# First stage of a hybrid encoder kernel: a hand-set order on four engines, and norm weights spread by a product with ones

## Chip, cores and metric

One core of a Trainium2 chip. The metric is the device time of one execution in microseconds; lower is better. The time before is the median of three runs.

## What is computed

Two layers over 512 tokens of width 1024, float32. Each layer normalises x, projects it to 4040 columns, runs four head groups on them (latent attention, differential attention, sparse attention, short convolution), gates them and projects back. Cut to what the change touches:

```python
def _rmsnorm(x, g):
    y = x * rsqrt(mean(x * x, axis=-1) + 1e-6)
    return y * g

for l in range(2):
    h = _rmsnorm(x, norm_g[l])
    p = split(h @ w_in[l])          # first: a_cq 256, a_ckv 128, a_krope 32, and c_kidx 32, c_widx 8
    ...
    x = x + y @ w_out[l]
return _rmsnorm(x, final_g)
```

## The kernel before

Tokens lie in 4 tiles of 128 (t = 0 to 3), the 1024 features of x in 8 groups of 128, taken in pairs (q = 0 to 3, one pair of weights each). Nearly all products are done in three passes of a split float32 (a high part `wh` or the first half of a `big`, and a low part `wl`): the high part is a copy on ACT, the low part a subtraction. For weights, `split_w` copies on ACT (L106) and subtracts on DVE (L108) and POOL (L101); for what leaves PSUM, `split_ps` copies on ACT (L115) and subtracts on DVE (L116). A PSUM bank is free again after DVE's part.

The first stage of a layer computes 456 columns (`a_cq`, `a_ckv`, `a_krope`, `c_kidx`, `c_widx`) for all tiles; the latent attention and the index scores wait for them. Its steps are listed in the string `FIRST`, one word each:

- `l`t loads tile t of x (two DMAs for tile 0; for tile 0 the norm weights too, L245, 512 KB: the row of 1024 weights is read for each of the 128 partitions into `g0`), all on SP's queue.
- `w`q loads weight group q, `c`q splits it (`first_load`, `first_split`).
- `s`t squares tile t on ACT in two halves with a sum (L261), `n`t finishes the norm: a root on ACT (L278), five small steps on DVE (L279 to L283), then x * scale * g in two halves on DVE (L286).
- `e`t transposes the normalised tile on PE, 8 transposes in 4 banks of two (L302, tag `pt`, 2 banks), each evicted by L115 and L116 (`Hidden.fill`).
- two digits, `qt`, are 6 products of 456 columns for group q and tile t (`first_part`); with q = 3 the norms of the latent vectors of tile t follow (`first_norm`, L527 to L537).

The set `START` names the engines on which the instructions of this stage keep the order of the code in the first layer: only SP. On the others a scheduler sets the order, within a model of its own, and it may bring in what comes later in the program. ACT, DVE, PE and POOL each run their queue in order. A root on one element (L994, `warm`) stands ahead of the stage in the code.

After the stage come the full projections (128 columns of the output at a time, 24 products of 512 columns each, L127), mixed with the latent products.

Of the kernel before, what the change touches and what calls it, by code (L numbers as in the profile page):

```python
# [9 lines left out]
FT = mybir.dt.float32  # L10
# [3 lines left out]
AF = mybir.ActivationFunctionType  # L14
# [5 lines left out]
P = 128  # L20
S = 512
D = 1024
# [4 lines left out]
EPS = 1e-6  # L27
BIG = 1e30
MARK = -3e38
FIRST = ("l0 w0 l1 l2 w1 l3 w2 w3 s0 n0 s1 c0 e0 00 n1 s2 c1 e1 01 10 11 n2 s3 e2 c2 02 12 20 21 n3 e3 c3 03 13 22 23 30 31 32 33",  # L30
         "w0 w1 c0 c1 00 10 01 11 w2 w3 c2 c3 e2 20 30 02 12 21 31 e3 03 13 22 32 23 33")
NBIG = 20
PIECE = 256
# [8 lines left out]
SLOTS = ('qi ga0 bl ga1', 'is|bi df0 gb0', 'sp1 tb', 'sp0 gc0 gb1 df1', 'tc cv0', 'cv1 gc1', '')  # L42
PW = 9.0
INORDER = set()
START = {mybir.EngineType.SP}
FM = (456, 456)
LATE = ((3, 3),)
FW = (("wh", "wl"), WB)
# [17 lines left out]
def hybrid_trunk(ctx, tc, x_in, norm_g, w_in, qa_g, w_uq, kva_g, w_ukv, dlam, subg,  # L66
                 conv_w, w_out, rel_bias, final_g, c_oh, c_cosf, c_sinf, c_tok, c_ones, c_mask, out):
    nc = tc.nc
    sb = lambda name, bufs: ctx.enter_context(tc.tile_pool(name=name, bufs=bufs))
    const = sb("const", 1)  # L70
# [7 lines left out]
    sm = sb("small", 4)  # L78
# [3 lines left out]
    def bank(tag):  # L82
        return ps.tile([P, 512], FT, name=f"ps_{tag}", tag=tag, bufs=BANKS[tag])

    def big(dt=FR):
        return pb.tile([P, 2, 512], dt, name="big", tag="big")

    def flat(t):
        return t.rearrange("p a b -> p (a b)")

    def prob():
        return pp.tile([P, 512], FT, name="prob", tag="prob")

    def raw_tile():
        return pw.tile([P, 1024], FT, name="wr", tag="wr", bufs=WR)
# [55 lines left out]
    ident = const.tile([P, P], FT, name="ident")  # L151
# [91 lines left out]
    def load_g(src, g=None):  # L243
        g = flat(big(FT)) if g is None else g
        nc.sync.dma_start(g, src[None, :].to_broadcast([P, D]))  # L245
        return g

    class Norm:


        def __init__(self, x, g, early=False):
            self.x, self.g, self.early = x, g, early
            self.xn = flat(big(FT))
            self.ss = sm.tile([P, 4], FT, name="ss")
            self.n = 0

        def part(self, c):
            n, ss = self.n, self.ss
            self.n += 1
            jk = prob()  # L260
            nc.scalar.activation(jk[:, :c.stop - c.start], self.x[:, c], AF.Square, accum_out=ss[:, n:n + 1])  # L261
            if c.stop < D:
                if n == 0:
                    nc.vector.tensor_scalar(out=ss[:, 0:1], in0=ss[:, 0:1], scalar1=1.0 / D, scalar2=EPS,
                                            op0=OP.mult, op1=OP.add)
                else:
                    nc.vector.scalar_tensor_tensor(out=ss[:, n:n + 1], in0=ss[:, n:n + 1], scalar=1.0 / D,
                                                   in1=ss[:, n - 1:n], op0=OP.mult, op1=OP.add)
            if self.early:
                for a in range(c.start, c.stop, PIECE):  # L270
                    d = slice(a, a + PIECE)
                    nc.gpsimd.tensor_tensor(out=self.xn[:, d], in0=self.x[:, d], in1=self.g[:, d], op=OP.mult)
# [36 lines left out]


    def layer(l, hT, enter, after):
        wl_ = w_in[l].rearrange("(k p) c -> p k c", p=P)
        pcl = lambda j: pcol[:, l * 10 + j:l * 10 + j + 1]
# [108 lines left out]
        def pair(k, unit, v, gt, post):  # L422

            yf = prob()
            for half in range(2):
                box = {}
                for j in range(2):
                    for qb in (2 * half, 2 * half + 1):
# [10 lines left out]
                        if qb % 2:  # L439
                            def prod(j=j, half=half, box=box):  # L440
                                nb = 2 * half + 2
                                if j == 0:
                                    box["o"] = bank("o")
                                o = box["o"]
                                pts = box[j]
                                for kb in range(nb):
                                    c = P if kb == nb - 1 else 0
                                    mm3(o[:, c:256], [tuple(x[:, kb, j * 64:j * 64 + P] for x in v)
                                                      + tuple(x[:, kb, c:256] for x in pts)],
                                        start=j == 0 and kb == 0, stop=j == 1 and kb == nb - 1, skip=True)  # L450
                                return 0.33 * nb

                            late.append((now + LAG[1], prod))
                            if j == 1:
                                c = slice(half * 256, (half + 1) * 256)
                                for i, part in enumerate(post(box, half, yf[:, c], gt[:, c])):
                                    late.append((now + LAG[2] + BSTEP * i, part))
                                if half == 1:
                                    late.append((now + LAG[2] + BSTEP * i, lambda: yfin(k, yf) or 0))
# [458 lines left out]

        with tc.manual_schedule(engines=START) if START and l == 0 else nullcontext():
            for step in FIRST[l].split():  # L920
                a, b = step
                if a == "w":
                    first_load(int(b))
                elif a == "c":
                    first_split(int(b))
                elif a in "lsne":
                    enter(int(b), a)
                else:
                    first_part(int(a), int(b))
            if l == 0:  # L930
                load_params()
# [56 lines left out]
        ctx.enter_context(tc.manual_schedule(engines=INORDER))  # L988
    h = Hidden()
    x0 = {}  # L990
    g0 = raw_tile()

    warm = sm.tile([P, 1], FT, name="warm", bufs=1)
    nc.scalar.activation(warm, ident[:, 0:1], AF.Sqrt)  # L994

    def enter(t, what, h=h):
        if what == "e":
            h.fill(t, x0[t].xn)
        elif what == "n":
            x0[t].finish()  # L1000
        elif what == "s":
            x0[t].part(slice(0, 512))
            x0[t].part(slice(512, D))
        else:
            x = flat(big(FT))
            for n in range(2 if t == 0 else 1):
                c = slice(n * 512, (n + 1) * 512) if t == 0 else slice(0, D)
                nc.sync.dma_start(x[:, c], x_in[t * P:(t + 1) * P, c])
            if t == 0:
                load_g(norm_g[0], g0)  # L1010
            x0[t] = Norm(x, g0)

    for l in range(DEPTH):
        st = {"n": []}

        def after(t, c, x, l=l, st=st):
            if t == 0 and c.start == 0:
                st["g"] = load_g(final_g) if l + 1 == DEPTH else load_g(norm_g[l + 1], raw_tile())
                if l + 1 < DEPTH:
                    st["h"] = Hidden()  # L1020
            if c.start == 0:
                st["n"].append(Norm(x, st["g"], l + 1 == DEPTH))
            norm = st["n"][t]
            norm.part(c)
            if c.stop < D:
                return
            norm.finish()
            if l + 1 < DEPTH:
                nc.sync.dma_start(xs[t * P:(t + 1) * P, :], x)
                if t >= 2:  # L1030
                    st["h"].fill(t - 2, st["n"][t - 2].xn)
            else:
                for c in (slice(0, 512), slice(512, 1024)):
                    nc.sync.dma_start(out[t * P:(t + 1) * P, c], norm.xn[:, c])

        layer(l, h, enter, after)
        if l + 1 < DEPTH:
            h = st["h"]

            def enter(t, what, h=h, ns=st["n"]):  # L1040
                h.fill(t, ns[t].xn)
# [52 lines left out]
```

## Time and profile before

| | us |
|---|---|
| median of 3 runs | 682.03 (677.00 to 683.62) |
| profiled execution | 679.76 |
| its span | 678.0 |
| PE busy in the span | 622.1 |
| start of PE's first instruction | 13.84 |
| granted TensorE clock, mean | 0.99 |

The span runs from the first to the last instruction of the core; the execution's own time holds 1.8 us around it. Times in the timeline are us from the span's start, then the us that the row lasts; a row with "xN" is N instructions run after one another, and its time is the sum that they cover. A bracket says how long the engine sat idle ahead of the row and what released it. PE is the product engine (its rows' ends are modelled), ACT, DVE and POOL the three others that compute, SP the queue that issues the loads.

### The profile page before, as it was taken

Reading aid. Unit: us, or ns where it says so; the run is one execution under the profiler, and the core shown is the slowest. Engines: PE = TensorE matmul, PEld = TensorE weight load, DVE = VectorE, ACT = ScalarE, POOL = GpSimd, SP = SyncE. Lnnn points to the kernel's source line nnn. Section 1 sums busy time; section 2 is a strip of 40 time slices with the busy share of each in tenths; the row PEclk is TensorE's granted clock in tenths of the full one; section 3 lists DMA queues with packets and bytes.
Section 4 is the critical chain, followed back from the end, with each engine's and each line's share of the span. In section 5 each row is a group of like instructions: output and inputs, shape, how many; then the busy total and the mean of one; then the engine's idle time right before and its main releaser. Section 6 shows DMA issues by size and latency. Waiting matters only on the chain.

```text
span 678.0 us, 11037 instructions
## 1 busy us (share of the span) xinstructions
PE 622.1 (92%) x3599; PEld 533.6 (79%) x3607; DVE 487.4 (72%) x1441; ACT 364.6 (54%) x879; POOL 278.5 (41%) x408
## 2 busy tenths in 40 slices
PE   1999999789999898999989899999999999999994
PEld 1877787678789677899968687879878977789994
DVE  3767762599999796645395767779999959664536
ACT  6556583484552564554364566866545256355435
POOL 2375432315434343442431854242534344344255
PEclk9999999799999999999999999999999999999998
DMA  8446573763455411233253653457244641132203
GB/s 262 117 111 191 148 133 94 185 158 99 109 145 151 118 47 43 83 125 114 58 169 91 181 171 103 139 135 170 65 115 116 190 117 48 47 109 100 80 1 125
DMA packets 86697, 80.71 MB, mean 119 GB/s; under 512 B 7302, under 2 KB 73400, under 8 KB 86640
## 3 DMA queue, kind: packets, MB, share of 16 engines
q1 hardware_dynamic: 86640, 80.02, 42.4%
q8 instruction: 28, 0.46, 0.3%
q14 instruction: 29, 0.24, 0.1%
HBM read 65.22 MB, written 12.16 MB: 114 GB/s over the span
## 4 chain that ended last, share of the span: by engine, by line
PE 58%; DVE 26%; ACT 7%; DMA 5%; issue 2%; POOL 1%; SPq 0%; ACTq 0%; DVEq 0%; POOLq 0%
PE ps_proj L127 43%; PE ps_o L127 5%; DVE ia L595 5%; DVE m L594 4%; PE ps_pt L414 3%; PE ps_s L127 2%; DMA wr<-in_w_in_dram 2%; DVE ptl L116 2%; DVE big L119 1%; DVE ps_s L490 1%; ACT prob L478 1%; DMA big<-in_x_dram 1%; PE ps_pt L302 1%; ACT prob L482 1%; DVE ia L581 1%
## 5 line engine op out<-in xcount | busy, mean ns | idle before, releaser
L101 POOL TENSOR_TENSOR wl<-wr,wh 128x256 fp32r<-128x256 f32 (+1 forms) x304 | 226.8, 779 | 326.1 <-ACT wh L106 279.4
L127 PE MATMUL ps_proj<-big,wh 128*128 128x512 f32 x768 | 250.7, 401 | 2.1 <-DVE prob L472 1.0
L127 PE MATMUL ps_proj<-wh,big 128*128 128x256 f32 (+2 forms) x768 | 173.1, 310 | 4.6 <-DVE big L116 2.1
L127 PEld LDWEIGHTS ps_proj<-big,wh 128*128 128x128 f32 x768 | 138.8, 189 | 26.8 <-issue 1.5
L127 PE MATMUL ps_proj<-big,wl 128*128 128x512 f32 x384 | 151.7, 395 | 0.0
L127 PEld LDWEIGHTS ps_proj<-wh,big 128*128 128x128 f32 x768 | 129.9, 193 | 9.6 <-DVE big L116 2.6
L127 PE MATMUL ps_proj<-wl,big 128*128 128x256 f32 (+2 forms) x384 | 116.8, 304 | 0.0
L106 ACT CAST wh<-wr 128x1024 fp32r<-128x1024 f32 (+2 forms) x84 | 83.8, 999 | 43.2 <-PE ps_proj L127 20.6
L127 PEld LDWEIGHTS ps_proj<-big,wl 128*128 128x128 f32 x384 | 72.3, 188 | 14.2
L127 PEld LDWEIGHTS ps_proj<-wl,big 128*128 128x128 f32 x384 | 74.4, 194 | 2.0
L116 DVE TENSOR_TENSOR ptl<-ps_pt,pth 128x128 fp32r<-128x128 f32 (+1 forms) x96 | 46.5, 485 | 31.4 <-ACT pth L115 30.8
L127 PE MATMUL ps_o<-pth,vt 128*128 128x256 f32 (+1 forms) x288 | 60.0, 280 | 5.2 <-ACT pth L115 3.9
L115 ACT CAST pth<-ps_pt 128x128 fp32r<-128x128 f32 (+1 forms) x96 | 40.5, 425 | 44.0 <-PE ps_pt L414 43.6
L478 ACT ACTIVATE prob<-ps_s,st_a 128x128 f32<-128x128 f32 (+1 forms) x64 | 33.8, 529 | 47.8 <-DVE st_a L490 30.7
L127 PEld LDWEIGHTS ps_o<-pth,vt 128*128 128x128 f32 x288 | 49.1, 194 | 10.0 <-ACT pth L115 6.5
L414 PE MATMUL ps_pt<-ident,prob 128*128 128x128 f32 x240 | 43.2, 278 | 10.2 <-ACT prob L482 7.1
L595 DVE MATCH_REPLACE8 ia<-m,ia 128x256 f32<-128x256 f32 (+2 forms) x96 | 52.0, 544 | 0.2
L594 DVE MAX8 m<-ia 128x8 f32<-128x256 f32 (+2 forms) x96 | 50.9, 550 | 0.1
L127 PE MATMUL ps_o<-ptl,vt 128*128 128x256 f32 (+1 forms) x144 | 42.3, 294 | 4.7 <-DVE ptl L116 4.7
L414 PEld LDWEIGHTS ps_pt<-ident,prob 128*128 128x128 f32 x240 | 28.5, 140 | 22.3 <-ACT prob L482 12.5
L482 ACT ACTIVATE prob<-prob,st_a 128x128 f32<-128x128 f32 (+1 forms) x64 | 35.8, 564 | 9.5 <-DVE st_a L481 9.3
L581 DVE SCALAR_TENSOR_TENSOR ia<-prob,widx,ia 128x256 f32<-128x256 f32 (+2 forms) x42 | 26.2, 639 | 12.7 <-ACT prob L576 12.0
(160 smaller groups left out, 949.1 us busy)
## 6 DMA issues: line engine op xcount, KB each, us to landing
wr<-in_w_in_dram SPq DMA_DIRECT2D x56, 512.0 KB
big<-trip SPq DMA_DIRECT2D x64, 128.0 KB
trip<-big SPq DMA_DIRECT2D x28, 256.0 KB
big<-in_x_dram SPq DMA_DIRECT2D x7, 512.0 KB
wr<-in_w_in_dram SPq DMA_DIRECT2D x8, 416.0 KB
big<-trip SPq DMA_DIRECT2D x32, 96.0 KB
wr<-in_w_out_dram SPq DMA_DIRECT2D x8, 384.0 KB
big<-big SPq DMA_DIRECT2D x8, 256.0 KB
```

Source lines behind the costliest of these rows:

```text
L101: nc.gpsimd.tensor_tensor(out=o[:, c], in0=a[:, c], in1=b[:, c], op=OP.subtract)
L106: nc.scalar.copy(h[:, :n], raw[:, :n])
L115: nc.scalar.copy(hi, src)
L116: nc.vector.tensor_tensor(out=lo, in0=src, in1=f(hi), op=OP.subtract)
L119: nc.vector.scalar_tensor_tensor(out=lo, in0=src, scalar=scale, in1=f(hi), op0=OP.mult, op1=OP.subtract)
L127: nc.tensor.matmul(o, lhsT=a, rhs=b, start=start and i == 0 and j == 0, stop=stop and i == n - 1 and j == 2, skip_group_check=skip)
L414: nc.tensor.transpose(b[:, k * P:(k + 1) * P], p[:, k * P:(k + 1) * P], ident)
L478: nc.scalar.activation(p[:, :W], s[:, :W], AF.Exp, scale=-1.0, bias=mn, accum_out=sums)
L482: nc.scalar.activation(p[:, :W], p[:, :W], AF.Copy, scale=st[:, 2:3])
L581: nc.vector.scalar_tensor_tensor(out=a, in0=r[:, :W], scalar=w, in1=a, op0=OP.mult, op1=OP.add)
L594: nc.vector.max(out=m8, in_=a)
L595: nc.vector.match_replace(out=a, in_to_replace=m8, in_values=a, imm_value=MARK)
```

## The change

Three things change. The string `FIRST` of the first layer is written in another order, and `START` now names ACT, DVE and PE beside SP, so that these four keep the order of the code in this stage. The norm weights of the first layer are loaded as one row on one partition and spread over the 128 partitions by two products with a column of ones on PE; ACT copies the results out of PSUM into `g0`, which moves from the buffers of raw weights to the `big` buffers. The dummy root moves from ahead of the stage to just before the squares of tile 0.

```diff
-FIRST = ("l0 w0 l1 l2 w1 l3 w2 w3 s0 n0 s1 c0 e0 00 n1 s2 c1 e1 01 10 11 n2 s3 e2 c2 02 12 20 21 n3 e3 c3 03 13 22 23 30 31 32 33",
+FIRST = ("l0 w0 l1 w1 l2 w2 l3 w3 s0 n0 c0 e0 s1 00 n1 c1 e1 s2 10 01 11 n2 c2 e2 s3 20 21 02 12 22 n3 c3 e3 30 31 32 03 13 23 33",
...
-START = {mybir.EngineType.SP}
+START = {mybir.EngineType.SP, mybir.EngineType.Activation, mybir.EngineType.DVE, mybir.EngineType.PE}
...
+            if self.warm and n == 0:
+
+                nc.scalar.activation(jk[:, 0:1], ident[:, 0:1], AF.Sqrt)
             nc.scalar.activation(jk[:, :c.stop - c.start], self.x[:, c], AF.Square, accum_out=ss[:, n:n + 1])
...
-    g0 = raw_tile()
-
-    warm = sm.tile([P, 1], FT, name="warm", bufs=1)
-    nc.scalar.activation(warm, ident[:, 0:1], AF.Sqrt)
+    g0 = flat(big(FT))
+    grow = const.tile([1, D], FT, name="grow")
+    one = const.tile([1, P], FT, name="one")
+    nc.vector.memset(one, 1.0)
...
             if t == 0:
-                load_g(norm_g[0], g0)
-            x0[t] = Norm(x, g0)
+                nc.sync.dma_start(grow, norm_g[0:1, :])
+                for n in range(2):
+                    b = bank("pt")
+                    nc.tensor.matmul(b, lhsT=one, rhs=grow[:, n * 512:(n + 1) * 512], start=True, stop=True)
+                    nc.scalar.copy(g0[:, n * 512:(n + 1) * 512], b)
+            x0[t] = Norm(x, g0, warm=t == 0)
```

How this moves instructions is seen on three engines. In the changed kernel the line numbers from the class `Norm` on are 3 higher, and 7 higher from the loads of x on.

ACT's queue from the start, before. L261 squares, L278 is the root of the norm, L106 copies a weight group, L115 evicts a transposed bank.

```order
L261 ACT_TABLE_LOAD
L261 ACTIVATE prob,ss<-big 128x512 x2
L278 ACT_TABLE_LOAD
L278 ACTIVATE nw<-ss 128x1
L106 CAST wh<-wr 128x912
L994 ACTIVATE warm<-ident 128x1
L261 ACTIVATE prob,ss<-big 128x512 x2
L278 ACTIVATE nw<-ss 128x1
L261 ACTIVATE prob,ss<-big 128x512 x2
L115 CAST big<-ps_pt 128x2x128
L106 CAST wh<-wr 128x912
L115 CAST big<-ps_pt 128x2x128
```

And after the change. L1017 copies the spread weights out of PSUM, L263 is the dummy root, L264 squares, L281 is the root.

```order
L1017 ACT_TABLE_LOAD
L1017 COPY big<-ps_pt 128x512 x2
L263 ACT_TABLE_LOAD
L263 ACTIVATE prob<-ident 128x1
L264 ACTIVATE prob,ss<-big 128x512 x2
L281 ACTIVATE nw<-ss 128x1
L106 CAST wh<-wr 128x912
L115 CAST big<-ps_pt 128x2x128 x4
L264 ACTIVATE prob,ss<-big 128x512 x2
L281 ACTIVATE nw<-ss 128x1
L106 CAST wh<-wr 128x912
L115 CAST big<-ps_pt 128x2x128 x4
```

The two copies now stand ahead of the squares of tile 0, and the squares of tiles 1 and 2 behind the four evictions of the tile before; the table loads are two, as before.

DVE's queue from its second instruction, before. L286 scales the tile, L264 is a step on the sums, L108 the low part of a weight group.

```order
L279 SCALAR_TENSOR_TENSOR nw<-ss 128x1
L280 RECIPROCAL nw<-nw 128x1
L281 TENSOR_TENSOR nw<-nw 128x1
L282 SCALAR_TENSOR_TENSOR nw<-nw 128x1
L283 SCALAR_TENSOR_TENSOR nw<-nw 128x1
L154 CAST identb<-ident 128x128
L108 TENSOR_TENSOR wl<-wr,wh 128x456
L264 TENSOR_SCALAR ss<-ss 128x1
L279 SCALAR_TENSOR_TENSOR nw<-ss 128x1
L280 RECIPROCAL nw<-nw 128x1
L286 SCALAR_TENSOR_TENSOR big<-big,nw,wr 128x512 x2
```

And after, where L289 scales the tile and L116 is DVE's part of an eviction.

```order
L283 RECIPROCAL nw<-nw 128x1
L284 TENSOR_TENSOR nw<-nw 128x1
L285 SCALAR_TENSOR_TENSOR nw<-nw 128x1
L286 SCALAR_TENSOR_TENSOR nw<-nw 128x1
L289 SCALAR_TENSOR_TENSOR big<-big,nw 128x512 x2
L108 TENSOR_TENSOR wl<-wr,wh 128x456
L116 TENSOR_TENSOR big<-ps_pt,big 128x2x128 x4
L267 TENSOR_SCALAR ss<-ss 128x1
L282 SCALAR_TENSOR_TENSOR nw<-ss 128x1
```

The scaling of tile 0 now follows its own small steps; the split of the weight group and tile 1's sums come behind it.

PE's queue from the start, before (L302 transposes, L127 is a product):

```order
L302 MATMUL ps_pt<-ident,big 128x128 x4
L127 MATMUL ps_proj<-wh,big 128x456
L127 MATMUL ps_proj<-wl,big 128x456
L302 MATMUL ps_pt<-ident,big 128x128 x2
L127 MATMUL ps_proj<-wh,big 128x456 x2
L302 MATMUL ps_pt<-ident,big 128x128 x2
```

And after, with the two products with ones in L1016 and the transposes in L305:

```order
L1016 MATMUL ps_pt<-grow,one 128x512 x2
L305 MATMUL ps_pt<-ident,big 128x128 x8
L127 MATMUL ps_proj<-wh,big 128x456
L127 MATMUL ps_proj<-wl,big 128x456
L127 MATMUL ps_proj<-wh,big 128x456 x2
L127 MATMUL ps_proj<-wl,big 128x456
L127 MATMUL ps_proj<-wh,big 128x456
L305 MATMUL ps_pt<-ident,big 128x128 x8
```

The eight transposes of a tile now stand together ahead of its products, where before products lay between them.

## Rows read from the trace of the kernel before

**Rows 1.** The page's part 1: busy us (share of the span), instructions.

```profile
PE 622.1 (92%) x3599; PEld 533.6 (79%) x3607; DVE 487.4 (72%) x1441; ACT 364.6 (54%) x879; POOL 278.5 (41%) x408
```

**Rows 2.** Waits of PE, 0 to 60 us: total us, times, longest.

```profile
PE ps_pt L302 <- DVE big L286: 13.8, 1, 13.8
PE ps_pt L544 <- DVE prob L621: 0.8, 1, 0.8
PE ps_proj L127 <- DVE big L537: 0.8, 1, 0.8
```

**Rows 3.** Busy us per engine in stretches; then PE clock, DMA share, GB/s.

```profile
45.60:60.00 14.40, 14.40 (x70) 11.18 (x70) 10.90 (x28) 8.61 (x14) 8.66 (x13) 1.00 0.65 181
```

**Rows 4.** Timeline 0 to 20 us, ACT, SP queue and POOL: start us, us, what.

```profile
0.74 0.85 SPq L1008 DMA_DIRECT2D big<-in_x_dram  x2
...
1.63 0.43 SPq L245 DMA_DIRECT2D wr<-in_norm_g_dram  x1
...
3.49 0.63 ACT L261 ACTIVATE prob<-big 128x512 f32<-128x512 f32 x1 [1.48 <-DMA big<-in_x_dram]
...
4.96 1.28 ACT L278 ACT_TABLE_LOAD   x1
...
6.26 0.29 ACT L278 ACTIVATE nw<-ss 128x1 f32<-128x1 f32 x1
...
9.82 0.95 ACT L106 CAST wh<-wr 128x912 fp32r<-128x912 f32 x1 [3.27 <-DMA wr<-in_w_in_dram]
...
10.86 1.73 POOL L101 TENSOR_TENSOR wl<-wr,wh 128x256 fp32r<-128x256 f32 x2 [9.09 <-ACT wh L106]
11.15 0.63 ACT L261 ACTIVATE prob<-big 128x512 f32<-128x512 f32 x1 [0.27 <-DMA big<-in_x_dram]
```

**Rows 5.** The same timeline, DVE, 6 to 22 us.

```profile
6.58 0.16 DVE L280 RECIPROCAL nw<-nw 128x1 f32<-128x1 f32 x1 [1.45 <-ACT nw L278]
...
7.17 0.16 DVE L283 SCALAR_TENSOR_TENSOR nw<-nw 128x1 f32<-128x1 f32 x1
...
10.81 0.63 DVE L108 TENSOR_TENSOR wl<-wr,wh 128x456 fp32r<-128x456 f32 x1 [3.34 <-ACT wh L106]
...
12.94 1.41 DVE L286 SCALAR_TENSOR_TENSOR big<-big,nw,wr 128x512 f32<-128x512 f32 x2
...
14.94 0.42 DVE L116 TENSOR_TENSOR big<-ps_pt,big 128x256 fp32r<-128x256 f32 x1
...
18.79 2.54 DVE L286 SCALAR_TENSOR_TENSOR big<-big,nw,wr 128x512 f32<-128x512 f32 x3
```

**Rows 6.** The same timeline, PE, 13 to 41 us.

```profile
13.84 1.09 PE L302 MATMUL ps_pt<-ident,big 128*128 128x128 f32 x4 [13.84 <-DVE big L286]
...
16.17 1.11 PE L127 MATMUL ps_proj<-wh,big 128*128 128x456 f32 x2
...
40.67 0.37 PE L127 MATMUL ps_s<-wh,big 128*128 128x456 f32 x1
```

**Rows 7.** Chain that ended last, 28 to 46 us: start us, us, what.

```profile
28.25 1.88 PE ps_proj L127 x9
30.12 0.44 PE ps_pt L302 x4
...
45.58 4.55 PE ps_proj L127 x20
```

**Rows 8.** Source view: fp32 product (L215), PSUM copy (L626).

```profile
L215 PE MATMUL ps_pt<-prob,rb x2: 481/484/488, 57.8 to 58.1; 32*12 32x384 f32 x2
...
L626 ACT CAST kst<-ps_pt x2: 581/584/587, 45.6 to 383.0; 128x512 fp32r<-128x512 f32 x2
```

**Rows 9.** Stretches again, in the second layer's first stage.

```profile
350.00:352.00 2.00, 0.00 (x0) 0.00 (x0) 2.00 (x4) 0.30 (x1) 2.00 (x2) 1.00 0.93 240
...
354.00:356.00 2.00, 2.00 (x7) 1.68 (x7) 1.34 (x7) 1.73 (x4) 0.00 (x0) 0.50 0.76 245
```

**Rows 10.** POOL's timeline, near 58 us.

```profile
58.17 2.82 POOL L101 TENSOR_TENSOR wl<-wr,wh 128x256 fp32r<-128x256 f32 x4 [5.02 <-ACT wh L106]
```

More of the change, by code (lines that the diff above doesn't have):

```diff
@@ L248, in hybrid_trunk, with __init__ @@
     class Norm:
-        def __init__(self, x, g, early=False):
-            self.x, self.g, self.early = x, g, early
+        def __init__(self, x, g, early=False, warm=False):
+            self.x, self.g, self.early, self.warm = x, g, early, warm
             self.xn = flat(big(FT))
```

## The prediction

> **What bounds the kernel now.** I read the page's first part, then the waits of PE in the first 60 us, then the timeline of every engine there. PE is busy 92% of the span [rows 1], so the question is what holds it up before it first runs and how densely it runs then. It waits 13.8 us at the start for L286, the scaled tile 0, and twice 0.8 us for the norms that follow the first stage [rows 2]; between 45.6 and 60 us it is busy all the time [rows 3]. Tile 0's own chain is short: x is there at 3.49 [rows 4], and its scale is finished by 7.33 (L283, 7.17 + 0.16) [rows 5]. L286 nevertheless starts at 12.94, because DVE's queue holds L108 (the split of weight group 0, whose data come at 9.82) and tile 1's sums (x of tile 1 comes at 11.15) ahead of it [rows 4, 5]. That is the wait that the change goes at. From 13.84 PE runs: transposes 0.27 us each [rows 6], later 0.11 (0.44 for 4); products of 456 columns first 0.4 apart, later 0.21 (1.88 for 9) [rows 6, 7]. The last product of the stage begins at 40.67 and ends at 41.04 [rows 6]. After it PE gets 8 products of 0.23, four transposes and the small parameter transpose done (2.5 us of work) until 45.58, from where it runs without a gap [rows 3, 7]: 4.54 - 2.5 = 2.0 us are lost there.
>
> **What the change does to the time, step by step.** All times count from the span's start; the profiled execution took 679.76 for a span of 678.0, and the median of the runs shown is 682.03, 2.27 above it. I add the difference found to that median. On PE the last 3,365 of 3,618 instructions stand in the same order as before, so everything after about 60 us should only be shifted.
>
> *Tile 0.* The 512 KB load of the weights becomes one row of 4 KB. No row shows such a load. x of tile 0 took 2.75 us from issue to use (0.74 to 3.49) and the weights' load is issued at 1.63 [rows 4]: 4.4, and I take 4.5; the ends are 3.5 (with x) and 5.6 (behind other loads). Then come two fp32 products of 512 columns. The only such product in the trace, of 384 columns, runs as two passes about 0.33 apart, 0.48 with the latency [rows 8]: 0.44 per pass of 512, four passes, 1.8 us at the full rate. PE's first work in the trace runs at half the later rate [rows 6, 7], so I take 3.5 us; 1.8 is the other end. ACT is kept in the written order, so its queue is copy, copy, table load, the dummy root, and only then the two squares of tile 0, which stood first before. First product ready 6.4, copy 0.58 [rows 8], second ready 8.1, copy to 8.7; table load 1.28 to 10.0; root 0.2; squares 1.47 (3.49 to the next row at 4.96); root 0.29: 12.0 [rows 4]. DVE's four small steps 0.75 (6.58 to 7.33): 12.7; PE's first transpose 0.9 after L286 starts (12.94 to 13.84) [rows 5, 6]: 13.6. The removed stall of L286 is thus eaten by the copies on ACT: 0.2 us gained, not 5.6. The new dummy root saves nothing: two table loads stood there before, and two stand there now.
>
> About that load the Trainium skill (ScalarE: Activation LUTs, "What ACT_TABLE_LOAD costs") counts 1.28 us for the load and 1.38 us more for a drain. The trace agrees with the first and shows no second part: the load of 4.96 ends at 6.24 and the root starts at 6.26 [rows 4]. By the page the step would end 1.4 us later; I use the rows.
>
> *Tiles 1 and 2.* Before, ACT squared tiles 1 and 2 while PE was idle or on tile 0. In the written order tile t's squares stand behind the four evictions of tile t-1, and L108 of its weight group stands ahead of its evictions on DVE. The loop that results, from the last eviction of one tile to the last of the next: squares 1.4, root 0.3, DVE's small steps 0.8, first half of L286 0.85 (three took 2.54 at 18.79, where POOL splits weights beside them; two took 1.41 at 12.94) [rows 5], then, with PE transposing the first half meanwhile, second half of L286 0.85, L108 0.8, and, since a PSUM bank comes free only after DVE's part, one DVE eviction 0.4, two transposes with latency 0.3, two copies on ACT 0.8 [rows 4, 5, 7]. Sum 6.5 us. PE has 8 transposes and 18 products in it, 0.9 + 3.8 = 4.7 us at full rate [rows 7]: it waits about 1.8 us in each. POOL's half of the split, 1.73 [rows 4], ends beside this. Tile 0's own evictions, with first transposes at 13.6 and L108 (0.65) in front, end at 16.6; so tile 1's end at 23.1 and tile 2's at 29.6.
>
> *The rest of the stage.* From 29.5 PE is the bound again: steps 20 to 22, 30 products, 6.3 us: 35.8. Tile 3 was scaled in the meantime (29.6 + 3.4), so its transposes cost only their two rounds through the banks, 1.3: 37.1. The last 42 products, 8.8: 45.9. Against 41.04 that is 4.9 later.
>
> *After the stage.* Tiles 0 to 2 now finish 5 to 8 us ahead of tile 3 (the order ends with 03 13 23 33), so their norms run while PE works, and the 2.0 us that PE lost there go. ACT now casts the next weights only at about 41 us, and POOL needs 0.75 us for each of four pieces; four groups in a row and the query weights follow. Before, POOL had idled 5.0 us ahead of the group at 58.17 [rows 10], so it can catch up; nothing is booked for this, with 2 us as the other end.
>
> *The clock.* The granted clock of TensorE falls from 2.4 to 1.2 GHz in this trace where PE idles: in the second layer, after a stretch with no PE work (350 to 352), it stands at 0.50 two microseconds later while PE is busy all the time [rows 9]. In the changed start PE runs the two products, idles some 5.5 us, then works in short bursts with waits of 1 to 2 us. I keep half rate up to tile 1's transposes, which costs nothing while PE waits anyway, and add 0.6 us: 18 products of tile 1 at half rate would cost 3.1, of which the 1.8 us of waiting swallow most, and I hold that for an even chance.
>
> The Trainium skill speaks against this change here (TensorE: Matmul & The Clock Gate, "HAM oscillation — how this bites in real kernels"): waits set between bursts of products bring the engine back to half rate burst after burst. The trace agrees as far as one idle stretch shows it [rows 9]; by the rule the even chance above would be a certainty, 0.7 us more.
>
> Sum: +4.9 - 2.0 + 0.6 = +3.5 us; 679.76 becomes 683.3, and set on the median of the runs shown 685.5.
>
> **Rivals.** *Slower by more: half rate lasts.* If the clock stays at 1.2 GHz into the 30 products after tile 2, each costs 0.17 more, 5.1 in all with nothing to hide it: 690.6. For it: the bursts; against it: PE has 3 to 4 us of unbroken work before. It decides from the point where those products begin at half rate. *Not slower: the start is early.* With the row there at 3.5 and the products at the full rate, tile 0 starts 2.7 us earlier; with DVE undisturbed by POOL the loop is 0.9 shorter, twice. The stage ends at 41.4, and with the 2.0 gained afterwards and no loss to the clock the kernel is 1.6 us faster: 680.4. For it: L286 also took 0.7 at times [rows 5]; against it: the half rate of all first work on PE [rows 6]. *POOL or the query weights come late* after 45 us: +2, 687.5. For it: the casts start only near 41 us; against it: POOL's idle time [rows 10]. *It does what it says*, and the engines overlap so that PE never waits after its start: transposes at 9 us, shortly after the scale that is ready at 7.33, then the stage in the 27.2 us that it took before (13.84 to 41.04): 4.8 gained there, 2.0 after it: 675.2. The written order of ACT speaks against it.
>
> **How the numbers follow.** A change below about 1% (6.8 us: 675.2 to 688.9) can't be told from none here. Chances: the forecast 0.50, lasting half rate 0.15, early start 0.20, late POOL 0.10, full gain 0.05. Slower by over 1%: most of the lasting half rate, and the upper tails of the forecast and of late POOL, 0.21. Faster by over 1%: the full gain and a little of the early start, 0.06. The rest, 0.73, is within 1%. The range of 680 to 691 runs from the early start to the lasting half rate.
>
> **What would show it.** Right: in the timeline ACT's squares of tile 0 start near 10 us behind copies and a table load; PE's first transpose lies between 12 and 14; PE waits in each of tiles 1 and 2 about 2 us, named as L286 and L116; the first stage's last product ends near 46; no wait for L537 or L621 follows. Wrong: squares at 4 us, a first transpose before 10, a first stage that ends before 42, or a different order of PE's time after 60 us.

## The result, and the profile after

The median is 684.35 us over 20 runs (681.6 to 689.13); the kernel before, run beside it, has 681.5 (677.0 to 686.4). The ratio is 1.0061, 95% interval 1.0043 to 1.0079: slower by 0.6%, which is less than the 1% set as the bound, and within 1.2 us of the forecast of 685.5. (The two medians alone are 2.85 us or 0.4% apart.) The profiled execution took 683.4 us with a span of 681.6, 3.6 more than before; the forecast was 3.5 more. The sum came out by luck: its terms did not, as the views show.

The waits of PE in the first 90 us answer to [rows 2] (Norm's lines are now 3 higher, those behind it too: L305 transposes, L289 scales, L547 and L624 were L544 and L621). Columns: engine, tile and line <- what ended the wait: us in total, times, longest.

```profile
PE ps_pt L305 <- DVE big L289: 7.3, 3, 5.5
PE ps_pt L1016 <- DMA grow<-in_norm_g_dram: 3.9, 1, 3.9
PE ps_pt L547 <- DVE prob L624: 1.8, 1, 1.8
PE ps_pt L417 <- ACT prob L485: 1.7, 1, 1.7
```

The one wait of 13.8 has become 3.9 for the row of norm weights and 7.3 for the scaled tiles. The wait for L537 is gone, but the one for the repeated key columns (L624) has doubled, and that of L417 grew from 1.2 to 1.7 us. ACT's timeline at the start (columns as in [rows 4]):

```profile
5.97 0.59 ACT L1017 COPY big<-ps_pt 128x512 f32<-128x512 f32 x1 [3.96 <-PE ps_pt L1016]
7.68 0.59 ACT L1017 COPY big<-ps_pt 128x512 f32<-128x512 f32 x1 [1.12 <-PE ps_pt L1016]
8.28 1.28 ACT L263 ACT_TABLE_LOAD   x1
9.58 0.20 ACT L263 ACTIVATE prob<-ident 128x1 f32<-128x1 f32 x1
9.81 0.63 ACT L264 ACTIVATE prob<-big 128x512 f32<-128x512 f32 x1
...
11.18 0.29 ACT L281 ACTIVATE nw<-ss 128x1 f32<-128x1 f32 x1
```

The squares of tile 0, whose data come near 3.5, start at 9.81, behind two copies, a table load and the dummy root. On DVE the small steps follow. These are its scaling of tile 0, its part of tile 0's evictions, and its scaling of tile 2:

```profile
12.28 1.89 DVE L289 SCALAR_TENSOR_TENSOR big<-big,nw 128x512 f32<-128x512 f32 x2
...
15.05 1.41 DVE L116 TENSOR_TENSOR big<-ps_pt,big 128x256 fp32r<-128x256 f32 x4
...
23.56 1.90 DVE L289 SCALAR_TENSOR_TENSOR big<-big,nw 128x512 f32<-128x512 f32 x2
```

PE's timeline shows what comes of it (it answers to [rows 6]):

```profile
3.90 3.75 PE L1016 MATMUL ps_pt<-grow,one 1*128 1x512 f32 x4 [3.90 <-DMA grow<-in_norm_g_dram]
13.18 2.16 PE L305 MATMUL ps_pt<-ident,big 128*128 128x128 f32 x8 [5.54 <-DVE big L289]
14.99 0.73 PE L127 MATMUL ps_proj<-wh,big 128*128 128x456 f32 x1
...
18.93 0.66 PE L305 MATMUL ps_pt<-ident,big 128*128 128x128 f32 x4 [1.31 <-DVE big L289]
20.07 0.66 PE L305 MATMUL ps_pt<-ident,big 128*128 128x128 f32 x4 [0.48 <-DVE big L289]
...
26.18 1.03 PE L305 MATMUL ps_pt<-ident,big 128*128 128x128 f32 x8
...
33.26 1.03 PE L305 MATMUL ps_pt<-ident,big 128*128 128x128 f32 x8
...
42.60 0.37 PE L127 MATMUL ps_s<-wh,big 128*128 128x456 f32 x1
```

The first transpose is 0.66 us earlier than before, PE waits 1.8 us for tile 1 and not at all for tiles 2 and 3, and the stage's last product ends at 42.97, 1.93 later than before. PE's clock in that stretch, in windows (us, then busy us and count of PE, PEld, DVE, ACT, POOL, then granted clock, DMA share, GB/s):

```profile
20.00:22.00 2.00, 1.83 (x8) 1.45 (x9) 2.00 (x6) 1.51 (x6) 0.48 (x1) 0.75 0.00 0
22.00:24.00 2.00, 2.00 (x7) 1.75 (x6) 1.60 (x8) 1.56 (x4) 0.33 (x1) 0.50 0.86 224
24.00:26.00 2.00, 2.00 (x11) 1.80 (x10) 2.00 (x3) 0.00 (x0) 1.94 (x2) 0.90 0.38 73
```

It falls to 1.2 GHz after the two waits of tile 1 and is back by 26. After the stage, DVE, then POOL and PE:

```profile
44.32 0.17 DVE L535 RECIPROCAL ssa<-ssa 128x2 f32<-128x2 f32 x1 [0.27 <-ACT ssa L533]
44.43 0.32 DVE L626 COPY widx<-t 128x32 f32<-128x32 f32 x1
44.66 0.76 DVE L536 TENSOR_TENSOR ssa<-ssa 128x2 f32<-128x2 f32 x1
45.35 0.82 DVE L649 TENSOR_TENSOR ropa<-t,ctok 128x64 f32<-128x64 f32 x1
46.09 0.69 DVE L537 SCALAR_TENSOR_TENSOR ssa<-ssa 128x2 f32<-128x2 f32 x1
46.71 0.41 DVE L624 COPY prob<-t 128x512 f32<-128x512 f32 x1
...
40.48 4.93 POOL L101 TENSOR_TENSOR wl<-wr,wh 128x256 fp32r<-128x256 f32 x7 [7.94 <-DVE ssa L532]
...
47.27 0.63 PE L547 MATMUL ps_pt<-ident,prob 128*128 128x128 f32 x4 [1.84 <-DVE prob L624]
```

L624 needs the 72 columns that ACT copies at 44.20 for 0.20 us, so it could start at 44.4; it starts at 46.71, behind three small operations with two inputs, on 2 or 64 numbers per partition, that take 0.69 to 0.82 us each while POOL splits weights. One of them (L536, L533 before) lasts 0.15 to 0.17 us in the kernel before as long as POOL is idle there (42.35 to 45.07) and 0.70 once POOL runs again:

```profile
42.84 0.16 DVE L533 TENSOR_TENSOR ssa<-ssa 128x2 f32<-128x2 f32 x1
...
45.91 0.70 DVE L533 TENSOR_TENSOR ssa<-ssa 128x2 f32<-128x2 f32 x1
```

The Trainium skill (SBUF — State Buffer, "SBUF: two separate sides") has a rule for that: a DVE operation with two SBUF inputs and a GpSimd operation hold one pair of ports in turn, each for a whole instruction. The rows agree: 0.7 us is what one of POOL's splits takes (4.93 for 7), and the reciprocal, with one input, keeps its 0.17. They do so in the main only: beside POOL a step with two inputs also took 0.31 (after, 40.93), and steps with one input 0.80 and 0.61 (before, 38.12 and 41.77).

How much later each instruction of PE is than the same one before (the order is equal from 45 us on, but for some products between 60 and 68):

| place in the kernel after, us | later by, us | what happened there |
|---|---|---|
| 42.6, end of the stage | 1.93 | see above |
| 48 to 62, 70 to 83 | 2.1 to 2.15 | wait for L624, 1.84, against 0.85 and 0.8 before |
| 84 to 120 | 2.7 | wait of L417, 1.69 against 1.17 |
| 130 to 228 | 2.45 | the clock falls in both kernels, at 121 before and at 123 after |
| from 233 to the end | 3.65 at the end, 3.75 to 4.1 up to 350 | the clock falls behind a wait of 2.15 us at 227.80; before, the same wait (2.16 at 225.35) has no fall |

The fall at 229: after, the wait, two products at 1.2 GHz and the window; then the wait and the window of before over the same work.

```profile
227.80 0.39 PE L763 MATMUL ps_s<-big 128*128 128x256 f32 x1 [2.15 <-DVE prob L773]
...
229.78 1.06 PE L127 MATMUL ps_proj<-big,wh 128*128 128x512 f32 x2
...
230.00:232.00 2.00, 2.00 (x7) 1.52 (x7) 0.50 (x2) 0.77 (x1) 1.15 (x2) 0.50 0.00 0
...
225.35 0.39 PE L760 MATMUL ps_s<-big 128*128 128x256 f32 x1 [2.16 <-DVE prob L770]
...
228.00:230.00 2.00, 1.91 (x11) 1.56 (x11) 0.83 (x5) 0.59 (x2) 1.71 (x3) 1.00 0.01 2
```

This fall moves PE by 1.3 us. Of the runs below, e2 to e5 have it in their profiles too, e1 and e6 to e8 don't; one profile of each doesn't show whether the change or chance brings it.

### The profile page after: what moved, and what is told of

The parts are those of the page before. It is cut to its first block, busy times and chain, and to the rows that moved or that the text cites. A ratio compares the mean times of both kernels' runs of the same rounds, so it can differ in the third digit from the quotient of the medians.

```text
span 681.6 us, 11055 instructions
## 1 busy us (share of the span) xinstructions
PE 627.9 (92%) x3611; PEld 536.7 (79%) x3611; DVE 493.5 (72%) x1442; ACT 365.2 (54%) x881; POOL 279.4 (41%) x408
## 5 line engine op out<-in xcount | busy, mean ns | idle before, releaser
L127 PE MATMUL ps_proj<-big,wh 128*128 128x512 f32 x768 | 252.3, 403 | 1.3 <-DVE prob L475 1.0
L127 PE MATMUL ps_proj<-wh,big 128*128 128x256 f32 (+2 forms) x768 | 173.3, 311 | 4.3 <-DVE big L116 2.2
L127 PEld LDWEIGHTS ps_proj<-big,wh 128*128 128x128 f32 x768 | 139.5, 190 | 26.6 <-DVE prob L475 1.4
L127 PE MATMUL ps_proj<-big,wl 128*128 128x512 f32 x384 | 152.3, 397 | 0.0
L127 PEld LDWEIGHTS ps_proj<-wh,big 128*128 128x128 f32 x768 | 130.4, 194 | 8.7 <-DVE big L116 2.4
L127 PE MATMUL ps_proj<-wl,big 128*128 128x256 f32 (+2 forms) x384 | 116.8, 304 | 0.1
L106 ACT CAST wh<-wr 128x1024 fp32r<-128x1024 f32 (+2 forms) x84 | 83.7, 998 | 38.6 <-PE ps_proj L127 17.8
L127 PEld LDWEIGHTS ps_proj<-big,wl 128*128 128x128 f32 x384 | 72.5, 189 | 14.3
L127 PEld LDWEIGHTS ps_proj<-wl,big 128*128 128x128 f32 x384 | 74.5, 194 | 2.4 <-DVE wl L108 0.4
L116 DVE TENSOR_TENSOR ptl<-ps_pt,pth 128x128 fp32r<-128x128 f32 (+1 forms) x96 | 46.5, 485 | 32.8 <-ACT pth L115 32.3
L127 PE MATMUL ps_o<-pth,vt 128*128 128x256 f32 (+1 forms) x288 | 60.0, 280 | 5.2 <-ACT pth L115 3.9
L115 ACT CAST pth<-ps_pt 128x128 fp32r<-128x128 f32 (+1 forms) x96 | 40.6, 425 | 45.0 <-PE ps_pt L417 44.6
L127 PEld LDWEIGHTS ps_o<-pth,vt 128*128 128x128 f32 x288 | 49.2, 194 | 10.0 <-ACT pth L115 6.5
L417 PE MATMUL ps_pt<-ident,prob 128*128 128x128 f32 x240 | 43.4, 280 | 10.7 <-ACT prob L485 7.6
L417 PEld LDWEIGHTS ps_pt<-ident,prob 128*128 128x128 f32 x240 | 28.8, 141 | 22.7 <-ACT prob L485 13.1
L127 PE MATMUL ps_o<-ptl,vt 128*128 128x256 f32 (+1 forms) x144 | 42.3, 294 | 4.7 <-DVE ptl L116 4.7
```

The costliest lines, as they stand in the source:

```text
L106: nc.scalar.copy(h[:, :n], raw[:, :n])
L115: nc.scalar.copy(hi, src)
L116: nc.vector.tensor_tensor(out=lo, in0=src, in1=f(hi), op=OP.subtract)
L127: nc.tensor.matmul(o, lhsT=a, rhs=b, start=start and i == 0 and j == 0, stop=stop and i == n - 1 and j == 2, skip_group_check=skip)
L417: nc.tensor.transpose(b[:, k * P:(k + 1) * P], p[:, k * P:(k + 1) * P], ident)
```

## Experiments

The theory (A): what ACT does ahead of tile 0's squares sets the start, and the stage is shifted with it; the written order itself costs nothing. Rivals: (B) the written order of the loop sets the end of the stage, so an earlier start gains nothing; (D) the clock does. For the wait behind the stage: (R) L624 stands too far back in DVE's queue, against the small operations being what everything waits for. Marks of all runs, in us of one profiled execution each; ratios are to the kernel before, run beside them, with 95% intervals.

| | first transpose | tile 1's | stage ends | wait for L624 (L621) | first 100x128 product | span | median | ratio |
|---|---|---|---|---|---|---|---|---|
| before | 13.84 | 20.01 | 41.04 | 0.85 | 76.52 | 678.0 | | |
| after | 13.18 | 18.93 | 42.97 | 1.84 | 78.67 | 681.6 | 684.35 | 1.0061 (1.0043 to 1.0079) |
| e1 | 9.60 | 15.15 | 38.91 | 1.89 | 74.60 | 675.4 | 680.83 | 0.9995 (0.9962 to 1.0028) |
| e2 | 11.90 | 18.87 | 40.15 | 0.85 | 75.65 | 683.2 | 679.99 | 0.9988 (0.9957 to 1.0019) |
| e3 | 10.35 | 16.09 | 39.82 | 1.85 | 75.52 | 678.0 | 680.25 | 1.0008 (0.9975 to 1.0041) |
| e5 | 14.43 | 20.47 | 43.93 | 1.88 | 81.22 | 687.3 | 685.6 | 1.0085 (1.005 to 1.012) |
| e4 | 8.10 | 14.33 | 38.39 | 1.84 | 74.05 | 676.8 | 678.48 | 0.998 (0.9965 to 0.9996) |
| e6 | 13.14 | 18.89 | 42.96 | none | 77.82 | 679.7 | 682.14 | 1.0026 (1.0007 to 1.0046) |
| e7 | 7.61 | 13.85 | 37.91 | none | 72.59 | 672.6 | 676.56 | 0.9941 (0.992 to 0.9961) |
| e8 | 8.23 | 14.17 | 38.63 | none | 73.83 | 675.8 | 677.22 | 0.9952 (0.9932 to 0.9972) |

**e1, the order alone.** The kernel after, with the 512 KB load back.

```diff
-                nc.sync.dma_start(grow, norm_g[0:1, :])
-                for n in range(2):
-                    b = bank("pt")
-                    nc.tensor.matmul(b, lhsT=one, rhs=grow[:, n * 512:(n + 1) * 512], start=True, stop=True)
-                    nc.scalar.copy(g0[:, n * 512:(n + 1) * 512], b)
+                load_g(norm_g[0], g0)
```

> The changed kernel with its hand-set order, but the norm weights come as the 512 KB load of before and no products or copies spread them. Theory A (the two copies and the table load that ACT must finish before it squares tile 0 hold up the start): the squares start at about 3.6 us instead of 9.81, tile 0's first transpose at 8.5 to 9.5 instead of 13.18, tile 1's at 15 to 16 instead of 18.93 (its x lands at about 11), the first stage ends near 39.6 instead of 42.97, and the span is some 3.4 us below the changed kernel's 681.6. Rival B (the order itself, with a tile's squares behind the evictions of the tile before, sets the end of the stage): the first stage ends within 1 us of 42.97 although tile 0 starts earlier, and the span stays at 680.5 or more.

The load is what tile 0's scaling now waits for, until 8.70:

```profile
8.70 1.42 DVE L289 SCALAR_TENSOR_TENSOR big<-big,nw 128x512 f32<-128x512 f32 x2 [1.85 <-DMA big<-in_norm_g_dram]
```

The first transpose (9.60) came just later than expected, the stage ended earlier (38.91 against 39.6), and the span is 6.2 below that of the kernel after, not 3.4: 4.06 of it stand at the stage's end, and the clock falls neither near 226 nor near 352 in this profile, as it does in the kernel after. Like e3, e4, e7 and e8 this run has one table load fewer.

**e2, the row and the products alone, in the order of before.**

```diff
-                load_g(norm_g[0], g0)
+                nc.sync.dma_start(grow, norm_g[0:1, :])
+                for n in range(2):
...
+                    nc.scalar.copy(g0[:, n * 512:(n + 1) * 512], b)
```

> The kernel of before with its scheduler's order, but with the row of 4 KB, the two products and the two copies. Theory A: the order there lets ACT square tile 0 first, so the spread costs nothing; the weights and tile 1 land about 1.2 us earlier, DVE's queue still holds the scaling of tile 0 behind tile 1's sums, the first transpose starts at 12 to 13 instead of 13.84 and the span is 0.5 to 1.5 us below 678.0. Rival C (the spread costs by itself, wherever it stands): first transpose after 14, span above 679.

The stage ends 0.89 earlier than before. The span is 5.2 longer all the same, for the clock falls oftener in this profile: the windows at 140 to 160, 220 to 240 and 580 to 600 us have 0.86, 0.91 and 0.91, where before has 1.00, and that at 340 to 360 has 0.85 against 0.91. The median equals before's. Rival C's span (above 679) is reached in this profile, its first transpose (after 14) is not: it starts at 11.90. ACT's timeline shows where the scheduler puts the copies: the squares first, at 3.46, and the second copy only at 8.66.

**e3, the copies behind the squares.** Products and copies stand behind tile 0's squares in the code; one table load fewer is left.

```diff
             x0[t].part(slice(512, D))
+            if t == 0:
+                for n in range(2):
...
+                    nc.scalar.copy(g0[:, n * 512:(n + 1) * 512], b)
```

> The changed kernel with the two products and copies written behind the squares of tile 0 (one table load fewer, since the first one then serves squares, copies and roots). Theory A: squares at 3.6, the copies end at 8.3 as the products do not move, the root of tile 0 follows at 8.3, tile 0's first transpose at about 10.3 instead of 13.18, tile 1's at about 16 instead of 18.93, stage end about 40.0 instead of 42.97, span about 678.7. Rival B: the stage ends at 42 or later, span 680.5 or more.

First transpose, tile 1 and end of the stage lie 2.8, 2.8 and 3.15 us before those of the kernel after. e1 and e3 speak for A: with the same written order the stage ends 3 to 4 us earlier as soon as ACT squares at 3.5. They refute B as it was put: from tile 1's transposes to the end of the stage it is 23.7 to 23.8 us in both, 24.0 in the kernel after.

That the written order itself costs nothing does not hold, though. From the first transpose to the stage's end it is 27.2 us before and 28.25 in e2, both in the scheduler's order, but 29.3 to 30.4 in all the others. So the stage of the kernel after ends 1.93 later although it begins 0.66 earlier: it is 2.6 us longer. Of this the timeline shows 1.79 us of waits for tile 1 and 18 products at 5.70 us (20.48 to 26.18) that take 3.8 at the full rate (0.21 each); what before loses in their place was not taken apart. Each part of the change by itself ends the stage earlier (e1 by 2.13, e2 by 0.89), both together later, since only then do the copies stand ahead of the squares.

**e5, PE kept busy.** Four unused products of the row before tile 0's transposes, two before tile 1's.

```diff
         if what == "e":
+            if t < 2:
+                b = bank("o")
+                for n in range((4, 2)[t]):
+                    nc.tensor.matmul(b, lhsT=one, rhs=grow[:, :512], start=True, stop=True)
             h.fill(t, x0[t].xn)
```

> The changed kernel with four more fp32 products of 512 columns on PE between the spread and tile 0's transposes and two more ahead of tile 1's, into a bank that nobody reads: PE has less idle time in the first 20 us. Theory D (part of what the changed kernel loses is TensorE's clock at 1.2 GHz, 21.0 to 24.2 us in the trace): with PE kept busy the 18 products after tile 1's transposes run at 0.21 us each instead of 0.38, the stage ends 1.2 to 2 us earlier (41 to 41.8), span 680 or less. Rival: the added products take PE's time themselves and the stage ends at 42.5 or later.

The added products, tile 0's and tile 1's transposes, and two windows:

```profile
7.47 7.03 PE L1004 MATMUL ps_o<-grow,one 1*128 1x512 f32 x8
14.43 1.97 PE L305 MATMUL ps_pt<-ident,big 128*128 128x128 f32 x8
...
20.47 1.36 PE L305 MATMUL ps_pt<-ident,big 128*128 128x128 f32 x8
...
22.00:24.00 2.00, 2.00 (x6) 1.73 (x6) 1.68 (x8) 1.97 (x8) 0.00 (x0) 0.50 0.32 66
...
50.00:52.00 2.00, 2.00 (x6) 1.62 (x5) 1.90 (x5) 0.00 (x0) 1.56 (x3) 0.50 1.15 331
```

The first eight added passes run at 0.88 us each, about as the first four (0.94), although PE has worked without a gap since 3.92. PE waits for neither tile now, and the clock still falls at 22 to 24, and once more behind the wait for L624: a wait is not what the first fall needs. The stage ends 0.96 later, as the rival said. D isn't borne out in this form: with such products in place of the waits the clock falls all the same, and they take PE's time. What the clock's fall costs the stage this run does not show.

**e4, the copies behind the root.** As after, but ACT's copies are issued inside tile 0's norm, behind its root.

```diff
             nc.scalar.activation(r, b, AF.Sqrt, scale=1.0 / D, bias=a)
+            while spread:
+                nc.scalar.copy(*spread.pop(0))
...
-                    nc.scalar.copy(g0[:, n * 512:(n + 1) * 512], b)
+                    spread.append((g0[:, n * 512:(n + 1) * 512], b))
```

> The changed kernel, with ACT's two copies of the spread norm weights written behind the root of tile 0 (after its squares) instead of ahead of the table load. Theory (what ACT does ahead of the squares of tile 0 sets the start, and the stage is shifted by it): squares at 3.5, root near 5, copies from 6.0 and 7.7, DVE scales the first half of tile 0 at 6.6 and the second at 8.3; PE's first transpose near 7.5 (changed kernel 13.18), tile 1's transposes near 14.1 (18.93), the stage's last product ends near 37.5 (42.97), first product of 100x128 near 73.2 (78.67). Rival (the landing of the weights, of x or POOL's splits hold the later tiles, so that an earlier tile 0 gains nothing): tile 1's transposes not before 15, the stage's end not before 38.5, as with the order alone.

The two products began half a microsecond later than in the kernel after (4.42 against 3.90; the trace names no transfer for this wait, so whether the row came late stays open), and with them the marks of PE are 0.2 to 0.9 later than expected; against the kernel after they are 4.6 to 5.1 earlier. The rival's bounds (15 and 38.5) aren't reached, though the second only just.

**e6, L624 inside the stage's order.**

```diff
             nc.scalar.copy(t1[:, t], a[:, 384:456])
+            if l == 0 and t == NT - 1:
+                rep_copy()
...
-            rep = prob()
-            repv = rep.rearrange("p (t r c) -> p t r c", t=NT, r=4)
-            nc.vector.tensor_copy(repv, t1[:, :, None, 32:64].to_broadcast([P, NT, 4, 32]))
+            if l:
+                rep_copy()
+            rep = A["rep"]
```

> The changed kernel, with the copy of L624 (the repeated key columns, 128x512 on DVE) written right behind the copy of the 72 columns of tile 3 on ACT, inside the stage's own order. Theory (the wait of 1.84 us at 47.27 is DVE's queue: five small operations of 0.7 to 0.8 us beside POOL stand ahead of L624, whose input is there at 44.40): L624 starts near 44.5, the wait on its transposes is below 0.4 us, the first product of 100x128 comes near 76.8 (78.67); stage end unchanged at 42.97. Rival (the small operations themselves are what everything waits for): the wait goes to the transposes of the normed latents behind it, and the first product of 100x128 stays above 78.

DVE's row for the copy (L624 is L527 here), and PE's waits from 0 to 100 us:

```profile
44.40 0.56 DVE L527 COPY prob<-t 128x512 f32<-128x512 f32 x1 [0.38 <-ACT t L539]
...
PE ps_pt L305 <- DVE big L289: 7.3, 3, 5.5
PE ps_pt L1023 <- DMA grow<-in_norm_g_dram: 3.9, 1, 3.9
PE ps_pt L417 <- ACT prob L485: 2.0, 2, 1.7
PE ps_proj L127 <- DVE big L119: 0.3, 1, 0.3
PE ps_pt L215 <- DMA prob<-in_c_oh_dram: 0.2, 1, 0.2
```

The copy starts as soon as its input is there and the wait is gone; its transposes come 2.17 us earlier, the products behind them 1.85, the first 100x128 product only 0.85. More than half of the gain is taken back between 55 and 60 us, where PE now waits 0.35 us for evictions on DVE (L119) and 0.19 for a transfer. So R holds for the wait, and its size was too high by 1 us; the rival (above 78) is missed by 0.2.

**e7, e4 and e6 together, and e8, e1 and e6 together.** No code but that of the two.

> Both edits together (copies behind the root of tile 0, and L624 inside the stage's order). If both theories hold and do not touch each other: stage's end near 37.5, no wait over 0.4 us for L624, first product of 100x128 near 71.4; 7 us below the changed kernel at the same clock, near 674 to 675 for the span, 1% below the kernel before. Rival (what comes early at the start is lost again to falls of the clock later): the marks at 37.5 and 71.4 are reached, and the median is still within 0.3% of the kernel before.

> The written order alone (512 KB load of the norm weights as before, no products with ones), with L624 inside the stage's order. Expected from the run of the order alone (first transpose 9.60, stage's last product ends 38.54 + 0.37, first product of 100x128 at 74.60 with a wait of 1.89 for L624): same start and stage end, wait below 0.4, first product of 100x128 near 72.8. Rival: as above, the wait moves on and that product stays above 74.

```profile
3.55 0.63 ACT L266 ACTIVATE prob<-big 128x512 f32<-128x512 f32 x1 [1.32 <-DMA big<-in_x_dram]
...
6.01 0.58 ACT L285 COPY big<-ps_pt 128x512 f32<-128x512 f32 x1 [0.80 <-PE ps_pt L1027]
7.71 0.58 ACT L285 COPY big<-ps_pt 128x512 f32<-128x512 f32 x1 [1.12 <-PE ps_pt L1027]
...
7.61 1.11 PE L309 MATMUL ps_pt<-ident,big 128*128 128x128 f32 x4
9.14 1.12 PE L309 MATMUL ps_pt<-ident,big 128*128 128x128 f32 x4 [0.42 <-DVE big L293]
```

e7 squares at 3.55, copies as the products come, and PE transposes the first half of tile 0 at 7.61 without any wait behind its products. Its stage ends 5.06 us before that of the kernel after, its first 100x128 product comes 6.08 earlier, and the span is 9.0 shorter. The last 3 of these come later, where this profile has no fall of the clock near 226 and 352. By the median it is 0.6% below before (interval 0.4% to 0.8%), where the kernel after, measured at another time, is 0.6% above. The rival, that falls of the clock eat the gain, fails for it; the expected 1% below before isn't reached either, nor is 71.4 for the first 100x128 product (72.59). e8 comes within 0.7 us of its median without any product with ones, and its first 100x128 product, at 73.83, lies between theory and rival. e8 also shows how far a mark can be trusted: up to tile 3's columns it is e1, and its load landed 1.37 us earlier (7.33 against 8.70), its first transpose as much; the stage's end differs by 0.28.

## Why the prediction was right, point by point

- *Tile 0* was right in its mechanism and nearly in its size. Squares at 9.81, behind copies and table load (forecast near 10); transposes at 13.18 (13.6). The row landed 0.6 earlier (3.9 against 4.5); the two products took 3.75 us (3.5 booked, for half rate). "The stall of L286 is eaten by the copies on ACT" is shown by e1, without the copies, and e3, with them behind the squares: they start 3.6 and 2.8 us earlier.
- *The table load* took 1.28 us and the root followed 0.02 later, so the drain that the Trainium skill adds (ScalarE: Activation LUTs, "What ACT_TABLE_LOAD costs") is not seen here either.
- *Tiles 1 and 2* failed, in size and in one step. The loop was booked at 6.5 us, with a wait of 1.8 in each tile. For tile 1 PE waited 1.79, as booked, and the last evictions of tiles 0 and 1 lie 5.84 apart (16.46 to 22.30). For tile 2 PE did not wait. The step "since a PSUM bank comes free only after DVE's part" did not bind: the 8 transposes of tile 0 run in a row, and the first product behind them starts at 14.99, before DVE's first eviction (15.05). The code names two banks for the four pairs; why they did not hold PE up is not shown. The larger failure is the second wait: tile 2 is scaled from 23.56 to 25.46, while PE has tile 1's products until 26.18, because they run at half rate at first.
- *The rest of the stage* was booked behind tile 2's last eviction, 30 products from 29.5 on. They start at 26.97, before that eviction ends (28.42), as the first 12 (steps 20 and 21) read tiles 0 and 1: 2.5 us. Tile 3's transposes took 0.8 instead of 1.3. So the stage ends at 42.97, not 45.9, and the term +4.9 is +1.93.
- *After the stage* the -2.0 did not come. PE's waits before were 0.85 and 0.79, 1.6 in all and not 2.0; after, it is 1.84 in one. The step said that tiles 0 to 2 finish early and so the waits go; but the wait is for tile 3's columns, and DVE's operations for them now lie beside POOL's splits, which the new order moved there. "POOL late" was looked for in POOL's own queue, and its cost came through DVE. e6 shows that the place in DVE's queue makes this wait.
- *The clock* was booked at 0.6 for tile 1's products. It fell there (22 to 24), but from tile 1's transposes to the stage's end the kernel after takes only 0.28 us more than e1, where it does not fall; e3, 0.31 shorter, has the fall too. A further 1.3 came at 229, in a place that the change doesn't touch. By the rule of the Trainium skill (TensorE: Matmul & The Clock Gate, "HAM oscillation — how this bites in real kernels") the prediction would have made the fall certain. The waits in that section's example last 3 to 5 us, those for tile 1 here 1.31 and 0.48, so the rule was stretched. After, e3, e4, e6 and e7 have such waits and the fall; but e5 has the fall without a wait, and behind the same wait near 226 the clock fell in one kernel's profile and stayed in the other's. What makes it fall stays open.
- *PE's order* is the same from 68 us on, as said, and the table above holds the places where its lag changes.

So the forecast of +3.5 was met by 1.93 (stage) + 0.2 (L624) + 0.3 (up to 228) + 1.2 (from there to the end) = 3.6. That is luck: the stage was overpriced by 3, the gain behind it that was to balance this was not there, and a third of the measured sum is a fall of the clock at 229 that the forecast did not name. Of the signs named beforehand, the squares near 10 and the first transpose between 12 and 14 came; the wait in tile 2, the stage's end near 46 and the absence of a wait for L621 did not. The lasting half rate (690.6) did not come, and neither did the full gain; e4 and e7 show that a gain was within reach with the same products (0.2% and 0.6% below before), once ACT's queue is in another order and, in e7, L624 in another place.

## What to carry to other kernels

When an engine is taken out of a scheduler's hands, read its queue as a list: work that waits for a late input (here two copies) must not stand ahead of work whose input has been there for 6 us, and a table load behind it adds its 1.3 us. A wait behind a stage goes away only if the last tile's chain gets shorter, so follow that chain through every engine beside it. Take the gain of such an edit first at marks (first transpose, end of the stage), since 4 us of 680 hide in the run-to-run spread; and take the marks from more than one execution, since those of e1 and e8 differ by up to 1.4 us. And measure the parts of a change apart: here each shortens the way to the stage's end, and the two together lengthen it.

## What the runs showed of the hardware

- The mean granted clock differs between executions of one kernel, and the time with it. Beside e4 and e6 to e8 the kernel before took 677.8 to 679.3 us at a mean of 0.991 (seven runs) and 682.1 to 683.1 at 0.981 (three): some 4 us, as much as e1 gained at its start. So e1's median equals that of before although the marks of its stage and the first 100x128 product lie 2 to 5 us earlier: five of its ten runs had a mean of 0.977 to 0.979, against two of the 28 of before beside it. Whether the order brings this or chance is not shown.
- PE starts at half rate in every kernel looked at, also where the granted clock reads 1.00. In the kernel after, two products at 16.66 and 17.04 are 0.38 apart, as those at 0.50 are, and the window beside them says 1.00; at the full rate they are 0.21 apart [rows 7]. The trace's first record of the clock stands at 17.6 us there (18.9 in the kernel before); ahead of it the windows print 1.00 for want of a record. In e5 ten microseconds of fp32 products on one row, without a gap, did not end it.

```profile
16.66 0.58 PE L127 MATMUL ps_proj<-wl,big 128*128 128x456 f32 x1
17.04 0.58 PE L127 MATMUL ps_proj<-wh,big 128*128 128x456 f32 x1
...
16.00:18.00 2.00, 1.62 (x5) 0.89 (x3) 1.27 (x8) 1.97 (x6) 0.00 (x0) 1.00 0.47 131
```

- An operation of DVE with two inputs, on two numbers per partition, takes 0.16 us alone and mostly 0.66 to 0.76 beside POOL's splits. With L624 moved ahead of such operations (e6) the first 100x128 product came 0.85 us earlier.
